# Reordering the mixers of a two-block network: linear attention among the gates' products, neighbourhood attention among Fourier mixing, gates by tanh, and dilated attention by pairs of units

## The chip, the cores and the metric

The kernel runs on one core of one Trainium2 chip. The metric is the device time of one execution in microseconds. Three runs of the kernel before took 4348.62 to 4350.44 us, median 4348.97 us.

## The reference, cut to what matters

Two blocks follow each other on a sequence of 2048 tokens of width 1024, all in float32. The first block is run twice (two layers, each with its own weights, on the 2048 latent tokens and 256 context tokens); the second block is run once.

```python
# first block, one layer
h   = rmsnorm(x, norm_w) * (1 + scale) + shift               # 2048 latent + 256 context tokens
f, fg, nq, nk, nv, ng, gq, gk, gv, gg, zf, zb = split(h @ w_in)
na   = neighbourhood_attention(nq, nk, nv, ctx_k, ctx_v, rpb) # 6 heads, 8x16 window + 256 context keys
gla  = gla_out_norm(gla_scan(forward) + gla_scan(backward))   # 4 heads, chunks of 64, gate logsigmoid/16
four = real(fft2(f, over positions and channels)) @ w_four
x    = x + gate * (concat(four * silu(fg), na * silu(ng), gla * silu(gg)) @ w_out)
# second block
q, k, v, gate_b, u, v_a, gate_a = split(rmsnorm(x) @ w_in_2)
o = dilated_attention(rope(norm(q)), rope(norm(k)), v)        # 8 heads, 3 dilations 1, 4, 16, merged by log-sum-exp
x = x + concat(o * silu(gate_b), gmlp(u, v_a) * silu(gate_a)) @ w_out_2
x = x + sigmoid(rmsnorm(x) @ w_ple_gate + b) * (p @ w_ple_proj)
```

## The kernel before

Every product is done in float32 as three fp32r products of high and low halves (`MM3`). The program is a sequence of Python generators. Each `yield` is a step, and a caller interleaves the steps of two or three generators; the framework's scheduler then fixes one instruction order per engine, and each engine takes its instructions in that order. Tiles come from pools with a fixed number of buffers; the attention scores, transposes and outputs live in PSUM banks.

A layer of the first block runs in stages. `b1_inproj` does the input projection. `mixers` (line 1318) then starts `Gates.steps` (line 558), a generator of 54 steps in layer 1 and 48 in layer 2, each one 24 products of 128x256 (`gps`, line 578) followed by a Silu on ScalarE (line 580). In this kernel two gate steps are taken after each step of `fourier` (22 steps in layer 1, 19 in layer 2; its products are named `fps`). Then the linear attention `Gla.steps` runs, 114 steps: three steps make one loop for one direction and one tile of 128 tokens (`gc` cumulative gates, `gT` transposes, `ga` masked scores, `gu` state updates, `go` outputs, `gpt` the transposes of a finished tile). The remaining gate steps go among the first 15 of these. After them the gates' memory is released and the neighbourhood attention `na` starts, one of its steps beside each further step of linear attention. Three `na` steps make one unit (128 queries of a pair of heads: `sc` and `sl` scores, `pc` and `pl` transposes, `po` values). The `na` steps left over run beside `ple_proj` (`plt`, `plo`) and the loads of `w_out`, and `OutProj` follows.

In `b2_attn`, the second block's attention, a unit is 128 queries of a head pair; there are 38 units for each of 4 head pairs, 16 with dilation 1, 14 with dilation 4 and 8 with dilation 16. `scores` (line 1783) makes two products that fill the array (line 1796) and two half-height ones (line 1799) per unit or part of a unit; VectorE adds the mask and takes the extremum, ScalarE takes exp; `turned` transposes (`apt`), `values` multiplies by V (`apo`). `step` (line 1939) lets transposes trail scores by two units and values trail by two more. `gather` sends the statistics of two dilations through DRAM on SyncE's queue, and `combine` merges the three dilations, for three of the four head pairs on GpSimd.

Of the kernel before, what the change touches and what calls it, by code (L numbers as in the profile page):

```python
# [10 lines left out]
F32 = mybir.dt.float32  # L11
# [522 lines left out]
class Gates:  # L534
# [24 lines left out]
    def steps(s):  # L559
# [9 lines left out]
        for i, c in enumerate(s.order):  # L569
            h = H.pop(i)  # L570
            for b in range(3):
                st = ip.ev.tile([128, 512], F32, name="ev", tag="ev")
                for j in range(2):
                    ps = s.pp.tile([128, 256], F32, name="gps", tag="gps", bufs=s.nps)
                    n = 0
                    for k in range(8):
                        for x, y in MM3:
                            nc.tensor.matmul(ps.rearrange("p (t n) -> p t n", t=2), W[b][k][y][:, 128 * j:128 * j + 128], h[x][:, :, k], start=n == 0, stop=n == 23)  # L578
                            n += 1
                    nc.scalar.activation(out=st[:, 256 * j:256 * j + 256], in_=ps, func=AF.Silu)  # L580
# [242 lines left out]
class Gla:  # L823
# [6 lines left out]
    def __init__(g, K, A, l, S, p, pp, nps, need):  # L830
# [8 lines left out]
        g.nw = p.tile([128, 96], F32, name="nw")  # L839
        nc.sync.dma_start(g.nw, dap(A["gla_norm_w"], 96 * l, [[0, 128], [1, 96]]))  # L840
        g.oacc = p.tile([128, 16 if not g.full else 18, 384], F32, name="oacc")
        g.L, g.VS, g.qd, g.kd = {}, {}, {}, {}
# [259 lines left out]
def na(K, A, l, S, B, p, pp, nps):  # L1102
# [99 lines left out]
    def turned(pr, g, j, st, es):  # L1202
# [6 lines left out]
        tcx = p.tile([128, 4, 128], F32, name="tcx", tag="tE", bufs=4)  # L1209
        nc.scalar.activation(out=tcx, in_=pc, func=AF.Copy)  # L1210
        tl = []
# [37 lines left out]
    def finish(pr, g, st):  # L1249
# [9 lines left out]
        ds = p.tile([8, 128], F32, name="ds", tag="ds", bufs=2)  # L1259
        if local:  # L1260
            nc.vector.tensor_copy(ds, dap_sb(pd, 127, [[-1, 128]]))
        else:
            nc.vector.tensor_copy(ds[:2 * n], pd[:2 * n])
        w = 128 * n
# [53 lines left out]
def mixers(K, A, l, S, B, ple, keep, proj):  # L1318

    tc = K.tc  # L1320

# [7 lines left out]
    with ExitStack() as es:  # L1329
# [7 lines left out]

        with ExitStack() as e1:
            for _ in fourier(K, A, l, S, pool(e1, "fo"), pool(e1, "fops", space=PSUM), 4):
                for _ in range(2):  # L1340
                    next(gates)
        w = proj.weights()
        with ExitStack() as e1:
# [3 lines left out]
            left = 3 * ((54 if l == 0 else 48) + 2)  # L1347
            for i, _ in enumerate(gla):
                if units is not None:
                    left -= 1  # L1350
                    next(units, None)
                elif i % 3 == 2 and [x for x in range(2) if next(gates, 1)]:
                    e2.close()
                    keep.close()
                    units = na(K, A, l, S, B, pool(es, "na", side="right"), pp, (2, 3))
                    next(units)
                    pp.tile = pool(es, "naps", space=PSUM, side="right").tile
        next(w)
        with ExitStack() as e1:
# [380 lines left out]
def b2_attn(K, A, S, p, pa, pq, pp):  # L1740
# [41 lines left out]

    def scores(pr, br, u, X):
        full = u[0][1] > 0
        st = X["st"]
        ps = pp.tile([128, 2, 512], F32, name="aps", tag="aps", bufs=2)
        ec = pa.tile([128, 2, 256], F32, name="ae", tag="ae", bufs=4)

        parts = [(u[0], u[0][1] - 1, slice(0, 256))] if full else [(x, 0, slice(128 * c, 128 * c + 128)) for c, x in enumerate(u)]

        early = (pr, br) == (0, 0) and u[0][1] < 4
        k0, q0, kl, k1, q1 = (K.first[:, i] for i in range(5)) if early else X["O"]
        for (r, b), b0, cs in parts:
            ks, qs = cols(br, r, b0, cs.stop - cs.start), cols(br, r, b, 128)
# [5 lines left out]
        for hh in range(2):  # L1800
            for (r, b), b0, cs in parts:

                col = (b, 4 * b + r, r)[br]
                m, d = (st[:, br, x, hh, col:col + 1] for x in range(2))
                nc.vector.tensor_tensor_reduce(out=ec[:, hh, cs], in0=ps[:, hh, cs], in1=band[:, cs if full else slice(128, 256)], scale=1.0, scalar=BIG,  # L1805
                                               op0=ALU.add, op1=ALU.min, accum_out=m)
                nc.scalar.activation(out=ec[:, hh, cs], in_=ec[:, hh, cs], func=AF.Exp, scale=-1.0, bias=m, accum_out=d)  # L1807
        return ec

    turn = [0]  # L1810

    def turned(pr, br, u, X, ec):
# [5 lines left out]
        et = pa.tile([128, 2, 2, 128], F32, name="aet", tag="aet", bufs=4)  # L1818
        turn[0] += 1
        if True:  # L1820
            nc.vector.tensor_copy(et[:, :, :n], pt[:, :, :n])
        else:
            nc.scalar.activation(out=et[:, :, :n], in_=pt[:, :, :n], func=AF.Copy)
        return et
# [22 lines left out]
    def gather(pr, X):  # L1847


        st = X["st"]  # L1850
        pst = pp.tile([64, 128], F32, name="pst", tag="apo", bufs=2)
# [3 lines left out]
        nc.vector.tensor_copy(sts, pst)  # L1855
        nc.sync.dma_start(sd[pr, 0].rearrange("s h (t n) -> (s h t) n", n=128), sts)
        for s_ in range(2):
            for hh in range(2):
                nc.sync.dma_start(dap(sd, ((pr * 2 + 1) * 4 + s_ * 2 + hh) * T, [[4, 128], [512, 4], [1, 4]]),
                                  st[:, 1, s_, hh].rearrange("p (b r) -> p b r", r=4))  # L1860
# [77 lines left out]

    def step(last=False):
        if len(B_) > 1 or last and B_:  # L1940
            last_, x = B_.pop(0)
            values(*x)
            if last_ and x[0] < 3:
                late.append(combine(x[0], x[3]))
        if len(A_) > 2 or last and A_:
            last_, x = A_.pop(0)
            B_.append((last_, x[:4] + (turned(*x),)))

    for i, (pr, br, n, u) in enumerate(units):
        X = Xs[pr]  # L1950
# [11 lines left out]
        if ahead and n % 2 == 0:  # L1962
            next(ahead, 1)
        A_.append((br == 2 and n == 7, (pr, br, u, X, scores(pr, br, u, X))))
        step()
# [6 lines left out]
    n = 0  # L1972
    while A_ or B_:
        step(True)
        if n < 3:
            next(last)
            n += 1
        yield
    yield True
# [409 lines left out]
```

## Time and profile before

| | us |
|---|---|
| median of 3 runs | 4348.97 |
| profiled execution, its own time | 4356.57 |
| its span, first to last instruction | 4354.8 |
| TensorE busy in the span | 4114.8 |
| VectorE busy | 1755.5 |
| ScalarE busy | 1649.8 |
| GpSimd busy | 1485.4 |

The mean granted TensorE clock is 0.956 of full speed. Busy time of TensorE is modelled, so a busy engine is not an engine at its peak. The profiled execution is 7.6 us above the median of the runs. In the rows below, PE is TensorE's products, PEld its weight loads, DVE VectorE, ACT ScalarE, POOL GpSimd, and times are counted from the start of the span.

### The profile page before, as it was taken

What the parts mean: (1) busy time and instruction counts of PE and PEld (TensorE: products, weight loads), DVE (VectorE), ACT (ScalarE), POOL (GpSimd) and SP (SyncE); (2) the same over time, 40 slices, a digit from 0 to 9 for tenths busy, and PEclk for the clock granted to TensorE, in tenths of its full rate; (3) what the DMA queues carried; (4) which work ended last, traced back from release to release, by engine and by line L of the source; (5) the groups of instructions that cost most, each with busy time, mean ns of one, the idle gap of its engine ahead of it and who ended that gap; (6) DMA issues with size and microseconds to landing.
All of it is one profiled execution on the core that took longest, in us unless ns stands there. A gap on an engine that the chain in (4) does not pass through costs nothing. (4 is left out here: it accounts for less than half of the span.)

```text
span 4354.8 us, 79569 instructions
## 1 busy us (share of the span) xinstructions
PE 4114.8 (94%) x29633; PEld 3510.3 (81%) x29633; DVE 1755.5 (40%) x4996; ACT 1649.8 (38%) x4121; POOL 1485.4 (34%) x1925
## 2 busy tenths in 40 slices
PE   7999999898899999999988989999999989998998
PEld 6988789676677799888967767889998867776887
DVE  5331123477532443112357744544620036665222
ACT  5141233574551333323355554251222125663121
POOL 4234333224222323232311422445723330643433
PEclk8999999898999999999989989999999988988999
DMA  6435444766766444434477674542321266745231
GB/s 206 138 112 150 145 162 152 190 166 182 201 188 209 140 142 126 123 120 158 150 201 178 165 203 153 170 126 76 107 89 50 87 194 141 174 107 162 84 92 63
DMA packets 551196, 629.94 MB, mean 145 GB/s; under 512 B 130792, under 2 KB 430124, under 8 KB 547354
## 3 DMA queue, kind: packets, MB, share of 16 engines
q1 hardware_dynamic: 500474, 477.71, 39.4%
q0 software_dynamic: 38784, 129.08, 9.0%
q10 hardware_dynamic: 11552, 18.08, 1.2%
q8 instruction: 235, 3.85, 0.4%
q14 instruction: 151, 1.24, 0.1%
HBM read 424.26 MB, written 200.41 MB: 143 GB/s over the span
## 5 line engine op out<-in xcount | busy, mean ns | idle before, releaser
L301 PE MATMUL mm<-whi,hTh 128*128 128x304 f32 (+2 forms) x1424 | 420.2, 299 | 1.6 <-ACT hTh L221 1.5
L301 PE MATMUL mm<-wlo,hTh 128*128 128x304 f32 (+2 forms) x1424 | 417.6, 297 | 0.0
L301 PE MATMUL mm<-whi,hTl 128*128 128x304 f32 (+2 forms) x1424 | 380.5, 296 | 0.0
L254 POOL TENSOR_TENSOR wlo<-wraw,whi 128x128 fp32r<-128x128 f32 (+3 forms) x384 | 223.7, 610 | 402.7 <-ACT whi L253 369.6
L301 PE MATMUL mm<-whi,h2h 128*128 128x256 f32 x1024 | 292.3, 289 | 1.5 <-ACT h2h L221 1.5
L301 PE MATMUL mm<-wlo,h2h 128*128 128x256 f32 x1024 | 284.2, 282 | 0.0
L301 PEld LDWEIGHTS mm<-whi,hTh 128*128 128x128 f32 x1424 | 268.9, 189 | 3.2 <-ACT hTh L221 2.3
L301 PE MATMUL mm<-whi,h2l 128*128 128x256 f32 x1024 | 271.1, 282 | 0.0
L301 PEld LDWEIGHTS mm<-wlo,hTh 128*128 128x128 f32 x1424 | 268.7, 189 | 0.0
L301 PEld LDWEIGHTS mm<-whi,hTl 128*128 128x128 f32 x1424 | 256.4, 189 | 1.1 <-issue 1.1
L578 PE MATMUL gps<-gh,whi 128*128 128x256 f32 x816 | 233.4, 286 | 8.5 <-ACT gh L155 8.5
L578 PE MATMUL gps<-gh,wlo 128*128 128x256 f32 x816 | 232.0, 284 | 0.0
L578 PE MATMUL gps<-gl,whi 128*128 128x256 f32 x816 | 231.5, 284 | 0.0
L304 PE MATMUL mm<-hTh,whi 128*128 128x512 f32 x600 | 227.9, 381 | 0.0
L304 PE MATMUL mm<-hTh,wlo 128*128 128x512 f32 x600 | 227.0, 378 | 0.0
L304 PE MATMUL mm<-hTl,whi 128*128 128x512 f32 x600 | 226.4, 377 | 0.0
L1430 PE MATMUL ops<-owh,omh 128*128 128x512 f32 x544 | 215.3, 396 | 4.2 <-ACT omh L155 4.2
L1430 PE MATMUL ops<-owh,om 128*128 128x512 f32 x544 | 213.0, 392 | 2.0 <-POOL om L156 2.0
L1430 PE MATMUL ops<-owl,omh 128*128 128x512 f32 x544 | 212.9, 391 | 0.0
L253 ACT ACTIVATE whi<-wraw 128x128 fp32r<-128x128 f32 (+3 forms) x416 | 127.3, 357 | 208.4 <-DMA wraw<-in_w_in 187.3
L1807 ACT ACTIVATE ae<-ae,ast 128x256 f32<-128x256 f32 (+1 forms) x384 | 171.1, 448 | 69.2 <-DVE ast L1805 69.2
L301 PEld LDWEIGHTS mm<-wlo,h2h 128*128 128x128 f32 x1024 | 195.7, 191 | 0.0
(483 smaller groups left out, 10893.4 us busy)
## 6 DMA issues: line engine op xcount, KB each, us to landing
qkv<-gl SPq DMA_DIRECT2D x72, 384.0 KB
adaw<-in_w_ada SPq DMA_DIRECT2D x48, 512.0 KB
Q<-ql SPq DMA_DIRECT2D x88, 256.0 KB
hl<-evk SPq DMA_DIRECT2D x68, 256.0 KB
gl<-hl SPq DMA_DIRECT2D x17, 1024.0 KB
om<-mixTl SPq DMA_DIRECT2D x34, 512.0 KB
gTl<-ev POOLq DMA_DIRECT2D x67, 256.0 KB, 3.1
wraw<-in_w_in SPq DMA_DIRECT2D x32, 512.0 KB
```

Of the source, the lines that this page charges most:

```text
L253: nc.scalar.activation(out=hi[:, :C], in_=raw[:, k], func=AF.Copy)
L254: (eng or nc.gpsimd).tensor_tensor(out=lo[:, :C], in0=raw[:, k], in1=f(hi[:, :C]), op=ALU.subtract)
L301: nc.tensor.matmul(ps[:, :C], s.hT[x][:, k, 128 * g:128 * g + 128], w[k][y][:, :C], start=st, stop=sp)
L304: nc.tensor.matmul(ps[:C, :tn], w[k][y][:, :C], s.hT[x][:, k, t0:t0 + tn], start=st, stop=sp)
L578: nc.tensor.matmul(ps.rearrange("p (t n) -> p t n", t=2), W[b][k][y][:, 128 * j:128 * j + 128], h[x][:, :, k], start=n == 0, stop=n == 23)
L1430: nc.tensor.matmul(ps, m[x][:, k], W[k][y][:, 512 * n:512 * n + 512], start=k == j == 0, stop=k == 7 and j == 2)
L1807: nc.scalar.activation(out=ec[:, hh, cs], in_=ec[:, hh, cs], func=AF.Exp, scale=-1.0, bias=m, accum_out=d)
```

## The change

Five things change. `Gates.steps` computes tanh(x/2) on ScalarE and then (tanh + 1) x on VectorE, which is twice the Silu; the factor one half is put into the linear attention's norm weight and into the neighbourhood attention's reciprocal denominators. In `mixers` the linear attention comes first with five gate steps for nine of its own, and the neighbourhood attention, begun when the gates are done, runs its steps beside the end of the linear attention, then beside Fourier mixing (4 steps per Fourier step in layer 1, 3 in layer 2), then beside `ple_proj`. While it is without linear attention (`K.alone`), one of its three evictions per unit goes to VectorE. In `b2_attn` two units share each pair of score tiles, all array-filling products stand before all half-height ones, and transposes and values follow by couples. The loads and stores of `gather` move from SyncE's queue to GpSimd's.

```diff
@@ Gates.steps
-                    nc.scalar.activation(out=st[:, 256 * j:256 * j + 256], in_=ps, func=AF.Silu)
+                    th = ip.ev.tile([128, 256], F32, name="gth", tag="ev")
+                    nc.scalar.activation(out=th, in_=ps, func=AF.Tanh, scale=0.5)
+                    nc.vector.scalar_tensor_tensor(out=st[:, 256 * j:256 * j + 256], in0=th, scalar=1.0, in1=ps, op0=ALU.add, op1=ALU.mult)
@@ Gla.__init__
+        nc.gpsimd.tensor_scalar(out=g.nw, in0=g.nw, scalar1=0.5, scalar2=None, op0=ALU.mult)
@@ na, turned
-        nc.scalar.activation(out=tcx, in_=pc, func=AF.Copy)
+        if K.alone:
+            nc.vector.tensor_copy(tcx, pc)
+        else:
+            nc.scalar.activation(out=tcx, in_=pc, func=AF.Copy)
@@ mixers
-        with ExitStack() as e1:
-            for _ in fourier(K, A, l, S, pool(e1, "fo"), pool(e1, "fops", space=PSUM), 4):
-                for _ in range(2):
-                    next(gates)
-        w = proj.weights()
+        K.alone = False
...
-                elif i % 3 == 2 and [x for x in range(2) if next(gates, 1)]:
+                elif i % 9 in (0, 2, 3, 5, 6) and next(gates, 1):
...
+        K.alone = True
+        w = proj.weights()
+        span = 4 if l == 0 else 3
+        with ExitStack() as e1:
+            for _ in fourier(K, A, l, S, pool(e1, "fo"), pool(e1, "fops", space=PSUM), 3):
+                for _ in range(span):
+                    left -= 1
+                    next(units, None)
@@ b2_attn, scores
-    def scores(pr, br, u, X):
+    def scores(pr, br, us, X):
-        ps = pp.tile([128, 2, 512], F32, name="aps", tag="aps", bufs=2)
+        ps = [pp.tile([128, 2, 256], F32, name="aps", tag="aps", bufs=4) for _ in range(2)]
...
+        for n, (i, _, (k0, q0, kl, k1, q1), r, b, cs, ks, qs) in enumerate(todo):
             for hh, (k, q) in enumerate(((k0, q0), (k1, q1))):
-                nc.tensor.matmul(ps[:, hh, cs], q[:, qs], k[:, ks], start=True, stop=False, skip_group_check=True)
+                nc.tensor.matmul(ps[hh][:, i, cs], q[:, qs], k[:, ks], start=n == 0, stop=False, skip_group_check=True)
+        for i, _, (k0, q0, kl, k1, q1), r, b, cs, ks, qs in todo:
             for hh, q in enumerate((q0, q1)):
                 h = slice(64 * hh, 64 * hh + 64)
-                nc.tensor.matmul(ps[:, hh, cs], q[h, qs], kl[h, ks], start=False, stop=True, skip_group_check=True)
+                nc.tensor.matmul(ps[hh][:, i, cs], q[h, qs], kl[h, ks], start=False, stop=True, skip_group_check=True)
@@ b2_attn, gather
-        nc.sync.dma_start(x, sd[pr].rearrange("b s h (i c) -> i (b s h) c", c=16))
+        nc.gpsimd.dma_start(x, sd[pr].rearrange("b s h (i c) -> i (b s h) c", c=16))
@@ b2_attn, step and its loop
-        if len(B_) > 1 or last and B_:
+        if B_:
...
-        if len(A_) > 2 or last and A_:
+        if len(A_) > 1 or done:
...
+        couple.append(u)
+        if n % 2:
+            A_.append((br == 2 and n == 7, [(pr, br, u, X, e) for u, e in zip(couple, scores(pr, br, couple, X))]))
+            couple = []
+            step()
-        if late and i % 2:
+        if late and n % 2 and (br or n > 5):
```

On ScalarE, in layer 1 where gate steps and linear attention run together, the kernel before has these rows (`ev<-gps` is the gate's Silu, `e<-gc` the linear attention's exp, `gT` its transposes):

```order
L580 ACT_TABLE_LOAD
L580 ACTIVATE ev<-gps 128x256
L934 ACT_TABLE_LOAD
L934 ACTIVATE e_8345<-gc 128x192
L935 ACTIVATE e_8346<-gc 128x192
L936 ACTIVATE e_8347<-gc 128x192
L941 ACTIVATE dec<-gc 48x2x2 x2
L1010 ACTIVATE oacc<-go 128x384
```

At such a place the changed kernel has these (`gth<-gps` is the gate's tanh):

```order
L965 ACTIVATE kT<-gT 128x256
L582 ACTIVATE gth<-gps 128x256
L155 ACTIVATE gh<-gl 128x1024 x2
L938 ACTIVATE e_6615<-gc 128x192
L939 ACTIVATE e_6616<-gc 128x192
L940 ACTIVATE e_6617<-gc 128x192
L945 ACTIVATE dec<-gc 48x2x2 x2
L582 ACTIVATE gth<-gps 128x256
```

The two table loads per gate step are gone from this place; the gate's tanh now stands between the exps of one loop and the copies of another.

On TensorE, in layer 1, the neighbourhood attention stands among the linear attention before:

```order
L1208 MATMUL pc<-ident,el 128x128 x4
L1217 MATMUL pl<-ident,el 80x128 x8
L1175 MATMUL sc<-Ks,Q 128x256
L1176 MATMUL sc<-Ks,Q 128x256
L1182 MATMUL sl<-Ks,Q 128x320
L1183 MATMUL sl<-Ks,Q 128x320
L1175 MATMUL sc<-Ks,Q 128x256
L1176 MATMUL sc<-Ks,Q 128x256
L975 MATMUL ga<-L_7910,kT 64x64 x8
L991 MATMUL gu<-qkv,ke 48x96 x8
L1235 MATMUL po<-tcx,vc 64x128 x2
L928 MATMUL gc<-la,tri 64x192 x4
```

In the changed kernel it stands among Fourier products (`fps`):

```order
L1186 MATMUL sl<-Ks,Q 128x440
L1212 MATMUL pc<-ident,el 128x128 x2
L1180 MATMUL sc<-Ks,Q 128x256
L1187 MATMUL sl<-Ks,Q 128x440
L1212 MATMUL pc<-ident,el 128x128 x2
L1242 MATMUL po<-tcx,vc 64x128 x4
L1265 MATMUL pd<-ident,dx 4x128
L750 MATMUL fps<-twh,ush 128x128 x2
L750 MATMUL fps<-twl,ush 128x128
L750 MATMUL fps<-twh,usl 128x128
```

The instructions of a unit are the same; what stands between them, and so what TensorE does while ScalarE and VectorE work on the unit, is other work.

On TensorE in the second block's attention the kernel before has these rows for the last unit of dilation 4 and the start of dilation 16 (`aps` scores, `apo` values, `apt` transposes); every unit of dilations 1 and 4 stands so:

```order
L1796 MATMUL aps<-kq 128x256 x2
L1799 MATMUL aps<-kq 128x256 x2
L1837 MATMUL apo<-aet,aV 64x128 x4
L1817 MATMUL apt<-ident,ae 128x128 x4
L1796 MATMUL aps<-kq 128x128 x2
```

The changed kernel has this for a couple of units of dilation 1:

```order
L1811 MATMUL aps<-kq 128x256 x4
L1815 MATMUL aps<-kq 128x256 x4
L1848 MATMUL apo<-aet,aV 64x128 x4
L1832 MATMUL apt<-ident,ae 128x128
L1848 MATMUL apo<-aet,aV 64x128 x4
L1832 MATMUL apt<-ident,ae 128x128 x7
```

The same products stand in groups twice as long, so there are half as many changes from one kind of product to the next.

## Rows read from the trace of the kernel before

**Rows 1.** Stage windows: length, then busy (count) of engines, clock, DMA share, GB/s.

```profile
core 0: us, PE busy (x) PEld busy (x) DVE busy (x) ACT busy (x) POOL busy (x), PEclk, DMA share, GB/s
578.00:747.00 169.00, 161.32 (x1258) 157.69 (x1258) 51.67 (x85) 65.00 (x139) 51.09 (x38) 0.96 0.52 168
800.50:822.00 21.50, 8.82 (x152) 6.61 (x152) 9.94 (x35) 7.96 (x22) 14.34 (x21) 0.88 0.90 204
822.00:1128.00 306.00, 278.79 (x3402) 224.09 (x3404) 213.01 (x792) 174.29 (x495) 100.18 (x136) 0.92 0.69 175
1128.00:1277.00 149.00, 130.00 (x1012) 101.61 (x1009) 61.54 (x198) 94.40 (x209) 17.86 (x24) 0.94 0.71 194
2202.60:2222.00 19.40, 13.08 (x185) 9.74 (x186) 11.55 (x36) 7.54 (x25) 8.83 (x15) 0.76 0.96 237
2222.00:2528.00 306.00, 273.61 (x3355) 221.79 (x3355) 204.48 (x767) 171.09 (x482) 94.41 (x128) 0.91 0.67 174
2528.00:2671.00 143.00, 121.83 (x902) 95.40 (x902) 56.80 (x178) 85.86 (x182) 14.86 (x19) 0.91 0.68 189
3555.00:3945.00 390.00, 378.38 (x2589) 286.74 (x2588) 240.72 (x952) 235.35 (x936) 136.00 (x157) 0.85 0.61 144
```

**Rows 2.** Windows, gate products (gps) on TensorE alone: busy (count), clock, DMA, GB/s.

```profile
747.00:763.00 16.00, 15.72 (x132) 1.00 0.77 254
784.90:799.20 14.30, 7.72 (x49) 1.00 0.72 210
```

**Rows 3.** Windows of the Fourier stages, Fourier products (fps) on TensorE alone.

```profile
578.00:747.00 169.00, 40.40 (x236) 0.96 0.52 168
2010.00:2156.00 146.00, 33.56 (x200) 0.98 0.54 173
```

**Rows 4.** Window 1177 to 1262: na transposes (pc), then ple products (plo), on TensorE.

```profile
1177.00:1262.00 85.00, 9.93 (x57) 1.00 0.71 191
...
1177.00:1262.00 85.00, 15.86 (x54) 1.00 0.71 191
```

**Rows 5.** The same window, all engines, columns as in rows 1.

```profile
1177.00:1262.00 85.00, 82.30 (x688) 65.82 (x687) 41.30 (x134) 62.94 (x137) 8.52 (x11) 1.00 0.71 191
```

**Rows 6.** Timeline, TensorE, a na unit's pieces: start, length, instruction [idle before].

```profile
2607.44 0.47 PE L1182 MATMUL sl<-Ks,Q 128*128 128x440 f32 x1
2607.75 0.37 PE L1183 MATMUL sl<-Ks,Q 128*128 128x440 f32 x1
2607.95 0.28 PE L1175 MATMUL sc<-Ks,Q 128*128 128x256 f32 x1
2608.07 0.28 PE L1176 MATMUL sc<-Ks,Q 128*128 128x256 f32 x1
2608.38 0.43 PE L1242 MATMUL po<-tl,vl 110*64 110x128 f32 x2
...
2609.82 1.09 PE L1242 MATMUL po<-tl,vl 110*64 110x128 f32 x14
2610.84 0.66 PE L1208 MATMUL pc<-ident,el 128*128 128x128 f32 x4
2611.33 1.04 PE L1217 MATMUL pl<-ident,el 128*110 128x128 f32 x8
2612.12 0.48 PE L1518 MATMUL plo<-plwh,plxsh 128*128 128x512 f32 x1
```

**Rows 7.** Groups by line, ScalarE: count, busy us, mean ns, idle before.

```profile
L1210 ACT ACTIVATE tcx<-pc 128x512 f32<-128x512 f32 x102 | 60.0, 588 | 34.0 <-PE pc L1208 33.9
L580 ACT ACT_TABLE_LOAD x8 | 10.3, 1283 | 0.1
L934 ACT ACT_TABLE_LOAD x7 | 9.0, 1283 | 2.6 <-PE gc L931 2.5
L936 ACT ACT_TABLE_LOAD x3 | 3.8, 1283 | 0.1
```

**Rows 8.** Timeline, TensorE, one unit of dilation 4 in the second block.

```profile
3793.62 0.66 PE L1817 MATMUL apt<-ident,ae 128*128 128x128 f32 x4
3794.03 0.81 PE L1796 MATMUL aps<-kq 128*128 128x256 f32 x2
3794.78 0.60 PE L1799 MATMUL aps<-kq 64*128 64x256 f32 x2
3795.30 0.66 PE L1837 MATMUL apo<-aet,aV 128*64 128x128 f32 x8
```

More of the change, by code (lines that the diff above doesn't have):

```diff
@@ L1259, in finish @@
         ds = p.tile([8, 128], F32, name="ds", tag="ds", bufs=2)
[L1260 to L1263, printed above, removed]
+        nc.vector.tensor_scalar(out=ds[:2 * n], in0=dap_sb(pd, 127, [[-1, 128]]) if local else pd[:2 * n], scalar1=0.5, scalar2=None, op0=ALU.mult)
         w = 128 * n
@@ L1781, in b2_attn @@
              [((r, 0), (r + 1, 0)) for r in range(0, 16, 2)]]
-    def scores(pr, br, u, X):
-        full = u[0][1] > 0
+    def scores(pr, br, us, X):
         st = X["st"]
-        ps = pp.tile([128, 2, 512], F32, name="aps", tag="aps", bufs=2)
[L1787 to L1794, printed above, removed]
+        ps = [pp.tile([128, 2, 256], F32, name="aps", tag="aps", bufs=4) for _ in range(2)]
+        ecs = [pa.tile([128, 2, 256], F32, name="ae", tag="ae", bufs=4) for _ in us]
+        todo = []
+        for i, u in enumerate(us):
+            full = u[0][1] > 0
+            parts = [(u[0], u[0][1] - 1, slice(0, 256))] if full else [(x, 0, slice(128 * c, 128 * c + 128)) for c, x in enumerate(u)]
+            early = (pr, br) == (0, 0) and u[0][1] < 4
+            O = [K.first[:, i] for i in range(5)] if early else X["O"]
+            todo += [(i, full, O, r, b, cs, cols(br, r, b0, cs.stop - cs.start), cols(br, r, b, 128)) for (r, b), b0, cs in parts]
+        for n, (i, _, (k0, q0, kl, k1, q1), r, b, cs, ks, qs) in enumerate(todo):
@@ L1800, in scores @@
-        for hh in range(2):
-            for (r, b), b0, cs in parts:
+                nc.tensor.matmul(ps[hh][:, i, cs], q[h, qs], kl[h, ks], start=False, stop=True, skip_group_check=True)
+        for i, full, _, r, b, cs, _, _ in todo:
+            for hh in range(2):
                 col = (b, 4 * b + r, r)[br]
                 m, d = (st[:, br, x, hh, col:col + 1] for x in range(2))
-                nc.vector.tensor_tensor_reduce(out=ec[:, hh, cs], in0=ps[:, hh, cs], in1=band[:, cs if full else slice(128, 256)], scale=1.0, scalar=BIG,
+                e = ecs[i][:, hh, cs]
+                nc.vector.tensor_tensor_reduce(out=e, in0=ps[hh][:, i, cs], in1=band[:, cs if full else slice(128, 256)], scale=1.0, scalar=BIG,
@@ L1806, in scores @@
                                                op0=ALU.add, op1=ALU.min, accum_out=m)
-                nc.scalar.activation(out=ec[:, hh, cs], in_=ec[:, hh, cs], func=AF.Exp, scale=-1.0, bias=m, accum_out=d)
-        return ec
-    turn = [0]
+                nc.scalar.activation(out=e, in_=e, func=AF.Exp, scale=-1.0, bias=m, accum_out=d)
+        return ecs
     def turned(pr, br, u, X, ec):
@@ L1818, in turned @@
         et = pa.tile([128, 2, 2, 128], F32, name="aet", tag="aet", bufs=4)
[L1819 to L1823, printed above, removed]
+        nc.vector.tensor_copy(et[:, :, :n], pt[:, :, :n])
         return et
@@ L1855, in gather @@
         nc.vector.tensor_copy(sts, pst)
-        nc.sync.dma_start(sd[pr, 0].rearrange("s h (t n) -> (s h t) n", n=128), sts)
+        nc.gpsimd.dma_start(sd[pr, 0].rearrange("s h (t n) -> (s h t) n", n=128), sts)
         for s_ in range(2):
             for hh in range(2):
-                nc.sync.dma_start(dap(sd, ((pr * 2 + 1) * 4 + s_ * 2 + hh) * T, [[4, 128], [512, 4], [1, 4]]),
+                nc.gpsimd.dma_start(dap(sd, ((pr * 2 + 1) * 4 + s_ * 2 + hh) * T, [[4, 128], [512, 4], [1, 4]]),
                                   st[:, 1, s_, hh].rearrange("p (b r) -> p b r", r=4))
         x = X["x"] = p.tile([128, 8, 16], F32, name="ax", tag="ax", bufs=1)
-        nc.sync.dma_start(x, sd[pr].rearrange("b s h (i c) -> i (b s h) c", c=16))
+        nc.gpsimd.dma_start(x, sd[pr].rearrange("b s h (i c) -> i (b s h) c", c=16))
     def combine(pr, X):
@@ L1937, in b2_attn, with step @@
     A_, B_, late = [], [], []
-    def step(last=False):
-        if len(B_) > 1 or last and B_:
[L1941 to L1944, printed above, removed]
-        if len(A_) > 2 or last and A_:
-            last_, x = A_.pop(0)
-            B_.append((last_, x[:4] + (turned(*x),)))
+    def step():
+        if B_:
+            last_, xs = B_.pop(0)
+            for x in xs:
+                values(*x)
+            if last_ and xs[0][0] < 3:
+                late.append(combine(xs[0][0], xs[0][3]))
+        if len(A_) > 1 or done:
+            if A_:
+                last_, xs = A_.pop(0)
+                B_.append((last_, [x[:4] + (turned(*x),) for x in xs]))
+    done, couple = [], []
     for i, (pr, br, n, u) in enumerate(units):
@@ L1963, in b2_attn @@
             next(ahead, 1)
-        A_.append((br == 2 and n == 7, (pr, br, u, X, scores(pr, br, u, X))))
-        step()
-        if late and i % 2:
+        couple.append(u)
[4 more added lines that the diff above has]
+        if late and n % 2 and (br or n > 5):
             if next(late[0], 1):
@@ L1972, in b2_attn @@
     n = 0
+    done.append(1)
     while A_ or B_:
[L1974 to L1978, printed above, removed]
+        step()
+        for _ in range(2):
+            if n < 3:
+                next(last)
+                n += 1
+            yield
     yield True
```

## The prediction

> **What bounds the kernel now.** I read the windows by stage first, then single pieces of work in the timeline, then the groups of ScalarE. The reader is to see in the windows that TensorE is busy for 161.3 of 169 us while Fourier products run among gate products, for 278.8 of 306 and 273.6 of 306 us while linear attention runs beside neighbourhood attention, and for 130.0 of 149 and 121.8 of 143 us in the stage beside the ple products; no other engine is over 213 of 306 [rows 1]. So TensorE's own work sets the time nearly everywhere, and reordering can only win what is idle (27, 19, 32 and 21 us in those four stages) and what runs at the lower clock: a mean grant of 0.92 means that 0.16 of a 306 us stage, 49 us, ran at 1.2 instead of 2.4 GHz. The second block's attention is busy 378 of 390 us at a grant of 0.85 [rows 1].
>
> I cut the mixers of layer 1 at 578 to 1277 us (699 us) and those of layer 2 at 2010 to 2671 (661 us), and rebuild each from prices.
>
> **Prices.** A gate product costs 16.0/132 = 0.121 us [rows 2]; a gate step has 24 of them. From 784.9 to 799.2 two loops of linear attention and 49 gate products took 14.3 us with almost no wait, so a loop costs (14.3 - 49 x 0.121)/2 = 4.2 us beside gates [rows 2]. Beside neighbourhood attention a step of linear attention, with the step of na next to it, took 306/99 = 3.09 us (114 steps less the 15 with gates) [rows 1]. Fourier's products are 40.4 and 33.6 us [rows 3]. A na unit beside ple: 57 transposes pc, four per unit, are 14.25 units in 85 us; less the 15.9 us in which ple products were busy, (85 - 15.9)/14.25 = 4.85 us, or 5.1 if a fifth of that time overlaps other work (an estimate) [rows 4]. Its pieces on TensorE alone add up to this: pc 0.49, pl 0.79, the 24 parts of po at 1.02 per 14 make 1.75, and two heads of scores sl and sc at 0.31 + 0.20 + 0.12 + 0.31 = 0.94 each make 1.88, in all 4.9 us; with the shortest of the score times, 0.2 and 0.12, it is 4.3 [rows 6]. So a unit costs at most 5.1 and at least 4.3 us, wherever it stands.
>
> **The mixers, stage by stage.**
> 1. Linear attention among gates. 54 gate steps at five of nine need 97 steps, 32.3 loops: 32.3 x 4.2 = 136 us, and 54 x 24 x 0.121 = 157 us. The transposes of finished tiles, which the priced window hasn't, and the start add 14 us (an estimate: the first stage was idle for 7.7 us before [rows 1], and now three loops of linear attention stand ahead of the first gate product, each waiting on ScalarE and VectorE). Layer 1: 307 us. Layer 2, 48 gate steps in 86 steps: 28.7 x 4.2 + 139 + 14 = 273.
> 2. The start of na, when its first loads wait for the gates' memory: 21.5 and 19.4 us before with TensorE busy 8.8 and 13.1 [rows 1]. It comes in the same place behind the last gate, so I keep 22 and 20.
> 3. Linear attention beside na: of 17 and 28 steps the first three lie in that start; 14 x 3.09 = 43 and 25 x 3.09 = 77 us.
> 4. na among Fourier: 88 and 57 steps are 29.3 and 19 units. The trace does not show this pair. Bounds are 4.3 and 5.1 us for a unit, with Fourier's products on top; I take 4.8, near the pieces' sum, since one eviction of 588 ns per unit leaves ScalarE [rows 7], which was busy for 62.9 of 85 us [rows 5]. 29.3 x 4.8 + 40.4 = 181 and 19 x 4.8 + 33.6 = 125 us.
> 5. na beside ple: 63 steps instead of 69 in layer 1, 65 instead of 51 in layer 2, and 0.3 us less for each unit: 149 - 10 - 6 = 133 and 143 + 22 - 6 = 159 us.
>
> Layer 1: 307 + 22 + 43 + 181 + 133 = 686 against 699. Layer 2: 273 + 20 + 77 + 125 + 159 = 654 against 661. Together 20 us less. That is little because the work is kept: what linear attention wins beside dense products, no wait and the full clock, is partly spent again where na loses its cover of gates.
>
> **Tanh.** 18 table loads of 1283 ns [rows 7] become two: 16 x 1.28 = 20.5 us of ScalarE. They lie in the stretch with gates, where TensorE had gate products to run, so I give them nothing; without this edit five gate steps among nine steps would have put a load before and behind nearly every one. New are 102 VectorE operations of 128x256 out of PSUM. The nearest row is a ScalarE eviction of 588 ns for twice the columns; at 0.3 to 0.6 us each they are 30 to 60 us on an engine that linear attention leaves mostly idle. They hold back the gate's PSUM bank, of which there are four; should that cover go, each gate step would wait for one such operation, 0.4 us, 41 us in all.
>
> By the Trainium skill (ScalarE: Activation LUTs, What ACT_TABLE_LOAD costs) a change of set costs 2.66 us with the drain that goes with the load. By that the removal would be 16 x 2.66 = 43 us of ScalarE, against 20.5 by the row; both are beside TensorE's work, so neither enters the sum.
>
> **The second block's attention.** In dilation 4 a unit takes 2.27 us: two array-filling products 0.75, two half-height ones 0.52, values 0.59, transposes 0.41, with no idle time between [rows 8]. All pieces stay. What can shrink is the half-height pair when another such pair follows it instead of the values: from 0.52 to at best the 0.375 of one array-filling product, 0.15 us per couple. A couple of full units has one such place (56 couples), one whose units have two parts has three (20 couples): 116 places x 0.15 = 17 us at best, nothing at worst. I take 8. The larger prize is the clock (a grant of 0.85 is 117 us at half speed), but the same products with the same strides give no reason for another clock; I give it nothing.
>
> By the Trainium skill (TensorE: Matmul & The Clock Gate, Part 3, what overlaps and what doesn't) a weight load overlaps a running product only when their row groups differ; pairs of half height that alternate between the upper and lower rows would then load under each other, and the 17 us would be had. The trace has no two such pairs in a row.
>
> Moving gather's DMAs to GpSimd puts them behind combine's products for the head pair before; the last combine waits for them. GpSimd is busy for 136 of 390 us in this stage [rows 1], so I cost it at nothing; if its queue is full just then, the length of a few of its operations, up to 10 us, appears in front of the tail's last products (an estimate).
>
> **Sum.** 20 + 8 = 28 us off the profiled execution's 4356.6. The median of the runs is 7.6 us lower; the same difference off 4349.0 gives 4321, and I say 4320.
>
> **Rivals.**
> A. The waits go as well. Beside Fourier's wide products na and linear attention keep the full clock, and idle time in the four na stages, 100 us in all, halves; a third of the 148 us that those stages spent at half speed is regained at half its length (25 us); couples get their 17 us. 4349 - 50 - 25 - 17 = 4257. For it: linear attention beside gates ran at a grant of 1.00 [rows 2]. Against it: idle time at the starts of stages has its own causes, loads behind released memory, and these remain.
> B. Nothing is left: na costs the full 5.1 us per unit beside Fourier and ple (0.3 x 91 units = 27 us back). 4349. For it: ScalarE, 63 of 85 us busy, gets Fourier's splits in addition.
> C. Slower: Fourier's chain becomes the wait. Each Fourier step loads, splits on ScalarE and then VectorE, and multiplies; TensorE takes its instructions in order, so a Fourier product whose half is late stops na too. Before, 48 independent gate products (5.8 us) stood between; now it is 1.3 units whose own exps sit ahead of the splits on ScalarE. At 2 us for each of the 41 Fourier steps this is 82 us: 4349 - 28 + 82 = 4403; from 0.7 us per step it eats the gain. Against it: before, this stage shows 7.7 us idle in all [rows 1].
> D. That the edit of the eviction does not do what it says (the wait moves with it from ScalarE to VectorE) is inside B.
>
> **How the numbers follow.** Forecast 0.50, with its own range 4285 to 4342; A 0.25; B 0.12; C 0.13, whose time is spread from 4350 upward. Two in ten left out at the ends gives 4245 to 4356: 0.09 below, out of A, and 0.10 above, out of C. A measurement of this kernel tells about 0.2%, 9 us: faster 0.77 (forecast nearly whole, A, a little of B), same 0.11, slower 0.12.
>
> **What would show it.** In the profile after: first stage near 300 us at a grant near 1.00, TensorE busy over 95%; no table loads between gates and exps; na among Fourier near 180 and 125 us. The clock in the second block's attention stays near 0.85 and the stage near 382 us. If Fourier products show long idle time before them, released by ScalarE or VectorE, it is C; if the na stages show under 5 us idle, A. The forecast is wrong if the first stage takes over 330 us: then linear attention's price beside gates was read from too short a stretch.

## The result and the profile after

The changed kernel takes 4376.73 us (median of four runs, 4370.39 to 4384.33) against 4348.8: 1.0061 of the time before, interval 1.0048 to 1.0074, so 28 us slower where 28 us faster was forecast. Its profiled execution took 4370.39 us, 13.8 more than that of before; it is the fastest of its four runs, while that of before lies above all its timed ones.

The stage windows of the changed kernel, columns as in [rows 1]; first layer 1 (start, linear attention among gates, start of `na`, linear attention beside `na`, Fourier, ple), then the same six of layer 2, then the second block's attention:

```profile
578.50:607.00 28.50, 15.25 (x157) 10.91 (x156) 12.40 (x34) 10.45 (x29) 5.02 (x13) 0.59 0.65 187
607.00:890.60 283.60, 274.45 (x3271) 244.22 (x3273) 175.27 (x537) 110.72 (x335) 119.38 (x128) 0.99 0.49 152
890.60:907.70 17.10, 9.82 (x139) 7.32 (x140) 11.21 (x44) 4.66 (x17) 9.92 (x16) 0.71 0.80 189
907.70:973.00 65.30, 44.98 (x422) 34.75 (x423) 31.17 (x126) 21.94 (x55) 28.16 (x38) 0.76 0.83 183
973.00:1163.50 190.50, 176.12 (x1418) 146.14 (x1417) 112.31 (x332) 109.94 (x255) 18.66 (x25) 0.93 0.66 183
1163.50:1302.30 138.80, 121.00 (x960) 94.31 (x958) 73.46 (x214) 80.33 (x178) 15.21 (x20) 0.93 0.71 195
2040.00:2068.80 28.80, 7.61 (x82) 4.82 (x81) 11.07 (x29) 5.89 (x13) 4.81 (x13) 0.58 0.69 191
2068.80:2312.20 243.40, 237.28 (x2817) 211.76 (x2818) 141.46 (x424) 96.83 (x293) 89.31 (x92) 0.99 0.49 152
2312.20:2330.00 17.80, 9.50 (x163) 7.26 (x162) 13.51 (x54) 5.68 (x20) 11.14 (x17) 0.94 0.78 180
2330.00:2419.00 89.00, 70.17 (x803) 57.44 (x804) 57.94 (x226) 42.41 (x112) 44.05 (x60) 0.88 0.84 205
2419.00:2551.50 132.50, 126.47 (x972) 104.44 (x972) 81.52 (x228) 78.24 (x179) 12.33 (x15) 0.92 0.75 204
2551.50:2694.90 143.40, 135.25 (x1103) 105.54 (x1103) 79.08 (x233) 88.00 (x192) 12.87 (x16) 0.99 0.69 199
3583.80:3960.20 376.40, 326.40 (x2573) 269.21 (x2573) 224.38 (x943) 228.22 (x933) 151.16 (x178) 0.87 0.59 147
```

Layer 1's mixers grew from 699 to 724 us, layer 2's fell from 661 to 655, and the second block's attention, 386 us from its first to its last product before, takes 376. The last stage of before, cut the same way, reads:

```profile
3557.00:3943.50 386.50, 375.73 (x2572) 284.55 (x2572) 238.48 (x944) 232.57 (x932) 133.57 (x154) 0.85 0.61 144
```

So TensorE is busy 49 us less than before, but idle for 50 of 376 us. Its timeline shows where: three long waits, at the end of three of the four head pairs.

```profile
3670.19 1.12 PE L1848 MATMUL apo<-aet,aV 128*64 128x128 f32 x8 [7.36 <-ACT aoT L1854]
...
3764.88 1.34 PE L1848 MATMUL apo<-aet,aV 128*64 128x128 f32 x10 [15.12 <-ACT aoT L1854]
...
3860.26 1.12 PE L1848 MATMUL apo<-aet,aV 128*64 128x128 f32 x8 [18.48 <-ACT aoT L1854]
```

ScalarE's eviction `aoT` is not the cause: ScalarE stood behind exps that waited for VectorE. VectorE's timeline has the cause, `combine`'s first minimum, idle before it for `gather`'s load `ax`:

```profile
3666.22 0.19 DVE L1883 TENSOR_TENSOR amn<-ax 128x32 f32<-128x32 f32 x1 [9.92 <-DMA ax<-sd]
...
3760.88 0.19 DVE L1883 TENSOR_TENSOR amn<-ax 128x32 f32<-128x32 f32 x1 [19.00 <-DMA ax<-sd]
...
3856.26 0.19 DVE L1883 TENSOR_TENSOR amn<-ax 128x32 f32<-128x32 f32 x1 [21.02 <-DMA ax<-sd]
```

Two things met. The load was issued late: for the second and third head pair its stores stand on GpSimd's queue behind `combine`'s products for the pair before, and for the first, when GpSimd was free, it stood idle for 6.18 us, which the profile's list of waiters puts down to `gather`'s own store. GpSimd's rows for the first and the second pair:

```profile
3659.54 0.94 POOL L1874 DMA_DIRECT2D ax<-sd  x1 [6.18 <-issue]
...
3746.66 1.28 POOL L1936 TENSOR_TENSOR aoT<-aoT 128x512 f32<-128x512 f32 x1
3747.88 0.80 POOL L1871 DMA_DIRECT2D sd<-ast  x1
```

And for these three pairs the scheduler put the minimum ahead of the masks of three of dilation 16's four couples, so that everything behind it on VectorE waited with it. For the second and third pair that place is not new: in the kernel before, all minima but the first stand ahead of six of dilation 16's eight units, and the second waited 1.55 us there:

```profile
3737.50 1.29 DVE L1871 TENSOR_TENSOR amn<-ax 128x32 f32<-128x32 f32 x1 [1.55 <-DMA ax<-sd]
```

Over the tile `ax`, who waited for it (us, times), in the changed kernel:

```profile
  DVE amn L1883: 53.7, 4
```

and in the kernel before:

```profile
  DVE amn L1871: 9.4, 3
```

The couples themselves gave far more than forecast. The same part of the timeline as [rows 8], one couple of dilation 4 (two units):

```profile
3642.32 1.29 PE L1811 MATMUL aps<-kq 128*128 128x256 f32 x4
3643.54 0.84 PE L1815 MATMUL aps<-kq 64*128 64x256 f32 x4
3644.31 1.09 PE L1848 MATMUL apo<-aet,aV 128*64 128x128 f32 x16
3645.34 1.09 PE L1832 MATMUL apt<-ident,ae 128*128 128x128 f32 x8
3646.18 1.29 PE L1811 MATMUL aps<-kq 128*128 128x256 f32 x4
```

From one couple's start to the next is 3.86 us, against 2 x 2.27 = 4.54 [rows 8]. Start to start, four array-filling products take 1.22 us (two took 0.75) and four half-height ones 0.77 (two took 0.52).

### The profile page after: what moved, and what is told of

The parts are those of the page before. It is cut to its first block, busy times and chain, and to the rows that moved or that the text cites. A ratio compares the mean times of both kernels' runs of the same rounds, so it can differ in the third digit from the quotient of the medians.

```text
span 4368.6 us, 79668 instructions
## 1 busy us (share of the span) xinstructions
PE 4079.7 (93%) x29633; PEld 3489.4 (80%) x29633; DVE 1841.1 (42%) x5188; ACT 1586.7 (36%) x4015; POOL 1501.6 (34%) x1951
## 5 line engine op out<-in xcount | busy, mean ns | idle before, releaser
L578 PE MATMUL gps<-gh,whi 128*128 128x256 f32 x816 | 242.3, 297 | 5.1 <-ACT gh L155 4.4
L1202 ACT ACTIVATE el<-el,st 128x696 f32<-128x696 f32 (+2 forms) x204 | 168.3, 826 | 109.1 <-DVE st L1199 107.0
```

Of the source, the lines that this page charges most:

```text
L1202: nc.scalar.activation(out=e[:, :n], in_=e[:, :n], func=AF.Exp, scale=-1.0, bias=m[:, hh, mi:mi + 1], accum_out=den[:, hh, dj:dj + 1])
```

## The experiments

All ratios are to the kernel before. "Layer 1" below is the length of layer 1's mixers in the run's profile, from the last input product to the first output product; before it was 699 us.

**Which edit costs: gather, attention, mixers, tanh.**

```diff
@@ e1_gather_sp: the changed kernel with
-        nc.gpsimd.dma_start(x, sd[pr].rearrange("b s h (i c) -> i (b s h) c", c=16))
+        nc.sync.dma_start(x, sd[pr].rearrange("b s h (i c) -> i (b s h) c", c=16))
...
@@ e2_b2_alone_sp: the kernel before with b2_attn of e1_gather_sp
@@ e3_mixers_alone: the changed kernel with b2_attn of before
@@ e4_tanh_alone: the kernel before with the diffs of Gates.steps, Gla.__init__ and na's ds
```

> The changed kernel with gather's loads and stores on SyncE's queue again, nothing else undone. Theory Q: in the changed kernel VectorE reached combine's first operation (amn<-ax) early and stood there 9.9, 19.0 and 21.0 us for gather's load behind GpSimd's queue, and TensorE lost 7.4, 15.1 and 18.5 us = 41 us to it. On SyncE those waits fall to the 1.6 to 6.3 us of the kernel before: 4377 - 41 + 2 = about 4338 us, second block's attention about 337 us. Rival P: the waits belong to the couples (two units' masks and exps stand ahead of each value product, whatever the queue): they remain, about 4377 us.

Measured 1.0006 (0.999 to 1.0022): 24 us less than the changed kernel. Theory Q holds in kind, not in size: VectorE waited 22.6 us for `ax` instead of 53.7, and the stage took 355.5 us, not 337. Of the four minima only the first now stood three couples later on VectorE, and the last two couples earlier; the second and third stood where they had, and waited 6.2 and 5.3 us for an earlier load instead of 19.0 and 21.0.

> The kernel before with the change of the second block's attention alone (couples, step, later combine), gather on SyncE's queue. Theory Q: the stage was 386 us before and 376 with 41 us of stalls after, so 335 us without them: 4349 - 51 = about 4298 us. Rival P: the stalls are the couples' own and stay, 4349 - 10 = 4339 us. Rival K (clock): the stage's half-speed time, 113 us before and 61 after, was shortened only because stalls broke the dense stretch up; without stalls it comes back, at half its length 26 us: about 4324 us.

Measured 0.9941 (0.9922 to 0.9961), 26 us faster; the stage took 357 us. That is nearest to K's number, but mostly not by K's mechanism: of the 22 us above theory Q's 335, 16 are idle time (25 us where Q left 50 - 41 = 9), and TensorE's busy time is only 5 us longer.

> The changed kernel with the second block's attention of the kernel before; so tanh and the new order of the mixers alone. Theory M: the order costs what the two profiles show between the start and that attention, 26 us, and all of it is the order's: 4349 + 26 = about 4375 us. Rival N: the profile of the kernel before was 7.6 us over its median and a good part of the shift is spread of single runs; the order costs under 10 us: 4349 to 4359 us.

Measured 1.0086 (1.0066 to 1.0106), 37 us slower; layer 1 took 734 us. Theory M, and more than the changed kernel's own profile showed: the same order took 734 to 736 us in three further profiles (gather on SyncE, the late minimum and the half-height products behind), so the 724 of the changed kernel's profiled execution is its low end.

> The kernel before with the gates' tanh and its halves alone; orders as before. Theory Z: the table loads lay beside gate products, so nothing changes: 4349, within 6 us. Rival L: the 18 loads of 1.28 us, less the two that stay, were in the path: 4349 - 20 = 4329 us. Rival V: each gate step now waits for the VectorE operation that follows, 0.4 us for 102 of them: 4349 + 41 = 4390 us.

Measured 1.0008 (0.9993 to 1.0022): nothing, as forecast.

**Where the mixers lose.**

```diff
@@ e5_silu: e1_gather_sp with Silu and whole factors
+                    nc.scalar.activation(out=st[:, 256 * j:256 * j + 256], in_=ps, func=AF.Silu)
@@ e6_tcx_act: e1_gather_sp with
-        K.alone = True
+        K.alone = False
@@ e7_layer2_only: e1_gather_sp with mixers of before where l == 0
@@ e8_gates_ahead: e1_gather_sp with, ahead of the loop over gla
+            for _ in range(6):
+                next(gates)
@@ e12_start_only: e1_gather_sp with, for l == 0, those six and
-                elif i % 9 in (0, 2, 3, 5, 6) and next(gates, 1):
+                elif i % 2 == 0 and next(gates, 1):
```

> The changed kernel with gather on SyncE (1.0006 of the kernel before in its own run) and with the gates' Silu and their whole factors instead of tanh; the order of the mixers is the changed one. Theory T: a gate step among linear attention's steps puts a table load of 1.28 us before and behind it on ScalarE, 2 x 102 at most, about 150 loads where exps and gates alternate; they hold the exps and transposes' copies that TensorE waits for, so at least a quarter, 50 us, shows: ratio 1.012 or more. Rival: TensorE has gate products to run meanwhile and nothing shows: 1.0006, within 0.002.

Measured 1.004 (1.0025 to 1.0056), 15 us over the same kernel with tanh. The profile has 114 of the loads at the two alternating lines:

```profile
L934 ACT ACT_TABLE_LOAD x57 | 73.1, 1283 | 3.9 <-PE gc L931 2.9
L580 ACT ACT_TABLE_LOAD x57 | 73.1, 1283 | 3.2 <-issue 2.4
```

146 us of ScalarE showed as about 15 in the time: between the two theories, a tenth and not a quarter.

> The changed kernel with gather on SyncE and the eviction tcx on ScalarE everywhere. Theory T: beside Fourier mixing and ple ScalarE was busy 110 of 190.5 and 72 of 116 us with that eviction on VectorE; 48 and 40 units there get 0.59 us more of it, and at the 0.3 us a unit of the prediction the four stages lose 0.3 x 91 = 27 us: ratio 1.007. Rival: the unit's wait only moves between the two engines: 1.0006, within 0.002.

Measured 1.0011 (0.9997 to 1.0026): the rival. Moving that eviction to VectorE is worth nothing that can be told.

> The changed kernel with gather on SyncE, and layer 1's mixers in the order of before (tanh kept). Theory L: the loss is layer 1's alone, where the mixers went from 699 to 724 us (734 in the two experiments on the order and on gather), while layer 2's went from 661 to 655: 25 to 35 us back, ratio 0.993 to 0.995. Rival S: both layers lose alike and the difference between the profiles is spread: half the 37 us of the mixers alone, ratio 0.996 to 0.998.

Measured 0.992 (0.9902 to 0.9938): theory L. Layer 1 took 697 us and layer 2 656. The loss is layer 1's alone.

> The changed kernel with gather on SyncE, and six gate steps taken before linear attention's first step, so that the three loops that stood uncovered at the start of each layer's mixers run among gate products; the rest of the order follows from that. Theory U: the starts, 28.5 and 28.8 us with TensorE busy 15.3 and 7.6 at a clock of 0.59 and 0.58, shrink by their idle time and their half speed, about 12 + 7 and 20 + 4 us, less one late loop's wait in each: 30 to 40 us, ratio 0.992 to 0.994. Rival W: the waits are for loads that come when they come, and the gates that cover them are missing at the end, where na starts earlier among more steps of linear attention: at best 10 us, ratio 0.998 to 1.001.

Measured 0.9968 (0.9957 to 0.9979), 17 us faster than without; layer 1 fell to 701 us, but layer 2 went from 653 to 658. Theory U's saving came in layer 1 alone, where the six steps do two things: they cover the start, and they leave ten more steps of linear attention for `na`. The next run parts them.

> The changed kernel with gather on SyncE (1.0006), and in layer 1 six gate steps ahead of linear attention's first step and the other 48 spread at one for two, so that nearly as many steps of linear attention as before stand among gates (96 of 97) and only the start is covered. Theory U: the uncovered start is the loss: layer 1's mixers fall from 734 to about 717 us, ratio 0.997. Rival W: what six gate steps ahead won (0.9968, layer 1 at 701 us) came from the ten steps of linear attention that moved beside neighbourhood attention, where they cost nothing: layer 1 stays at 725 to 735, ratio 0.999 to 1.001.

Measured 0.997 (0.9956 to 0.9985); layer 1 at 720 us, 15 less: theory U. By the profiles, the other 19 us that `e8_gates_ahead` won in layer 1 go with the ten moved steps. Its two windows of layer 1, up to the last gate and from the start of `na` on:

```profile
579.10:863.40 284.30, 267.18 (x3192) 238.34 (x3193) 166.98 (x494) 113.81 (x337) 109.16 (x120) 0.98 0.52 158
...
881.40:1279.90 398.50, 349.23 (x3009) 281.42 (x3009) 231.74 (x733) 219.84 (x516) 77.15 (x102) 0.94 0.73 195
```

and those of `e12_start_only`:

```profile
579.60:885.00 305.40, 283.96 (x3421) 251.85 (x3421) 183.26 (x569) 119.94 (x360) 121.07 (x139) 0.97 0.53 158
...
901.70:1299.20 397.50, 347.48 (x2796) 280.09 (x2796) 219.09 (x671) 212.17 (x488) 62.12 (x84) 0.89 0.71 187
```

With 213 more products of linear attention beside `na`, that part took 398.5 instead of 397.5 us, at a grant of 0.94 instead of 0.89; the part with gates was 21 us shorter for them. In this pair of profiles the ten steps are nearly free beside `na` and paid in full beside gates. The times do not confirm it: the ratios of the two runs, 0.9968 and 0.997, agree within their intervals, and with layer 2 some 5 us longer in `e8_gates_ahead` they leave about 6 us for the ten steps (an estimate), not 19. Layer 2's profiles say the opposite (`e13_start_layer2`, below).

**What stalls and what wins in the second block's attention.**

```diff
@@ e10_minima_late: the changed kernel with
-        nc.vector.tensor_tensor(out=m2, in0=x[:, 0, 0], in1=x[:, 1, 0], op=ALU.min)
-        nc.vector.tensor_tensor(out=m2, in0=m2, in1=st[:, 0, 0], op=ALU.min)
+        nc.vector.tensor_tensor(out=m2, in0=x[:, 0, 0], in1=st[:, 0, 0], op=ALU.min)
+        nc.vector.tensor_tensor(out=m2, in0=m2, in1=x[:, 1, 0], op=ALU.min)
@@ e11_half_behind: e1_gather_sp, the half-height pair inside the first loop of scores
-        for i, _, (k0, q0, kl, k1, q1), r, b, cs, ks, qs in todo:
             for hh, q in enumerate((q0, q1)):
```

> The changed kernel, gather still on GpSimd's queue, with combine's first minimum taken between dilation 16's statistics and gather's first load, so that VectorE meets it three couples of dilation 16 later. Theory V: GpSimd's queue alone does no harm, the harm was that VectorE came to the wait with masks behind it; of 41 us of waits at least 30 go, less what the half-speed clock takes back: 20 us or more, ratio 1.0015 or less. Rival Q: the queue itself makes combine late and TensorE waits for it at another place: 1.006.

Measured 0.9981 (0.9967 to 0.9995), 35 us less than the changed kernel, with `gather` still on GpSimd. Theory V: the stage took 347 us.

> The changed kernel with gather on SyncE (1.0006) and the half-height products of each part put behind its own array-filling ones again; couples of transposes and values stay. Theory G: what the couples won, 47 us of TensorE's time in the stage, is a price of each change between kinds of products; a couple of dilation 4 has 6 changes instead of 4 (8 before), one of dilation 16 has 10 instead of 4; half of the gain or more, 23 to 38 us, goes: ratio 1.006 to 1.009. Rival H: only pairs of half-height products under each other won, at most the 17 us of the prediction: ratio 1.002 to 1.0045. Rival F: the gain came from fewer waits and another clock: 1.0006.

Measured 1.0119 (1.0104 to 1.0134): 49 us over the same kernel with the half-height products apart, beyond theory G. Its stage:

```profile
3595.00:3992.20 397.20, 392.83 (x2572) 300.60 (x2572) 224.16 (x943) 227.91 (x931) 131.66 (x149) 0.84 0.57 139
```

Its pairs of scores in dilation 4 cost what they cost before, 0.73 and 0.53 us from start to start (0.75 and 0.52 in [rows 8]):

```profile
3644.40 0.80 PE L1811 MATMUL aps<-kq 128*128 128x256 f32 x2
3645.13 0.60 PE L1814 MATMUL aps<-kq 64*128 64x256 f32 x2
3645.66 0.84 PE L1811 MATMUL aps<-kq 128*128 128x256 f32 x2
3646.43 0.60 PE L1814 MATMUL aps<-kq 64*128 64x256 f32 x2
3646.96 0.88 PE L1831 MATMUL apt<-ident,ae 128*128 128x128 f32 x6
```

So the whole gain is the grouping of scores by kind; couples of transposes and values give nothing without it. The stage was even 11 us longer than before, with TensorE busy for 17 us more; no run explains that.

**The best of both.** `e9_both` is `e7_layer2_only` with the late minimum; the two runs behind it settle what was open.

```diff
@@ e13_start_layer2: e9_both with e12_start_only's edit where l == 1
@@ e14_best_gather_pool: e9_both with gather on nc.gpsimd
```

> The kernel with layer 1 in the order of before, layer 2 in the changed order and gather on SyncE (0.992 in its own run), and combine's first minimum taken between dilation 16's statistics and gather's first load instead of between gather's two: VectorE then cannot meet it before dilation 16's masks are done. Theory V: with gather on SyncE VectorE still stood 5.2, 6.2, 5.3 and 5.9 us for that load and TensorE about 17 us for VectorE; they go: 0.988. Rival: the transposes and values stand still for other reasons there, or the half-speed clock takes the place: 0.992.

Measured 0.9884 (0.9869 to 0.99), 50 us faster than the kernel before: theory V. Only the minimum differs from `e7_layer2_only`, whose stage took 353.6 us:

```profile
3562.70:3899.10 336.40, 322.89 (x2573) 266.16 (x2573) 223.73 (x943) 228.40 (x932) 132.31 (x149) 0.92 0.71 165
```

> The best kernel so far (layer 1 in the order of before, layer 2 in the changed one, gather on SyncE, the late minimum; 0.9884 in its own run) with layer 2's start covered as layer 1's was: six gate steps ahead of linear attention's first step, the other 42 at one for two (84 steps of linear attention among gates instead of 86). Theory U: the uncovered start costs layer 2 what it cost layer 1, 15 us: its mixers go from 656 to about 641 us, ratio 0.985. Rival E: the start costs layer 2 nothing, since what follows na's start was 5 us longer there for the six steps ahead while it was 33 us shorter in layer 1: 656 us, ratio 0.988.

Measured 0.9882 (0.9864 to 0.9899), layer 2 at 656 us: rival E. The part up to the last gate was 15 us shorter (255 against 270), and what follows 15 us longer (401 against 386). Why layer 2 gives it back and layer 1 doesn't, stays open. Its layer 2 up to the last gate, and from there on:

```profile
2002.60:2257.30 254.70, 237.88 (x2842) 212.16 (x2843) 143.60 (x439) 100.46 (x298) 88.45 (x100) 0.98 0.54 162
2257.30:2658.20 400.90, 354.85 (x3091) 282.60 (x3089) 232.82 (x754) 217.87 (x510) 85.32 (x113) 0.92 0.73 195
```

and that of `e8_gates_ahead`, which has the same six gate steps ahead in layer 2 and nine more steps of linear attention beside `na`:

```profile
2018.10:2258.20 240.10, 225.64 (x2636) 202.92 (x2637) 129.11 (x374) 95.12 (x277) 77.42 (x84) 0.98 0.53 158
2258.20:2676.30 418.10, 367.75 (x3298) 293.66 (x3297) 246.48 (x816) 223.20 (x534) 99.50 (x129) 0.91 0.74 195
```

The nine steps took 14.6 us off the part with gates and put 17.2 us on the part behind it: in layer 2 they were not free beside `na`.

> The best kernel so far (0.9884) with gather on GpSimd's queue, as in the changed kernel; so all of the change but the order of layer 1's mixers, plus the late minimum. Theory V: VectorE's place was the whole harm: 0.988 to 0.989. Rival Q: GpSimd's queue costs by itself what the attention stages of the two experiments with the late minimum differ by, 347 against 336 us: 0.991.

Measured 0.9886 (0.9869 to 0.9903): theory V. The attention stage took 343 us, 7 more than on SyncE, of which the time shows nothing.

## Why the prediction was wrong

**The mixers of layer 1: the failed step.** Forecast 307 + 22 + 43 + 181 + 133 = 686; the windows show 312 + 17 + 65 + 190.5 + 139 = 724. The price of linear attention beside gates held (312 against 307 us, 316 to 322 in four other profiles of this order), and the start of `na` took less than forecast. What failed first is step 3, 14 steps at a mean of 3.09 us. That mean was taken over 99 steps, and the first loops beside `na` cost more in both kernels. Linear attention's `gc` in two stretches before, the start of `na` and the even run behind it (16 products are one loop):

```profile
802.60:854.20 51.60, 6.02 (x64) 4.00 (x64) 4.46 (x20) 0.77 1.01 222
865.20:996.80 131.60, 19.14 (x258) 13.24 (x258) 17.83 (x80) 0.96 0.64 172
```

and the start of `na` after:

```profile
899.10:947.70 48.60, 3.08 (x34) 1.92 (x34) 2.23 (x10) 0.61 1.00 204
```

A loop took 12.9 us at the start and 8.2 in the even run; after, 24 us, at a grant of 0.61 and with the DMA engines at their full share. TensorE's longest waits there are for `na`'s first loads and for VectorE:

```profile
907.72 0.55 PE L1179 MATMUL sc<-Ks,Q 128*128 128x256 f32 x1 [4.28 <-DMA Q<-ql]
...
916.60 0.55 PE L1179 MATMUL sc<-Ks,Q 128*128 128x256 f32 x1 [5.27 <-DMA Ks<-kl]
...
942.72 0.56 PE L995 MATMUL gu<-qkv,ke 64*48 64x96 f32 x4 [7.47 <-DVE ggt L1041]
```

The cost of the first loops was averaged over 99 steps, and the mean was then applied to 14 steps that are mostly first loops. In step 4 a unit among Fourier products cost (190.5 - 40.4) / 29.3 = 5.1 us, the upper bound and not the 4.8 taken; the reason for 4.8, the eviction that leaves ScalarE, is worth nothing (`e6_tcx_act`). Step 5 missed by 6.

Behind these sums stands an idea that did not carry. The prediction called TensorE's work the limit and moved linear attention to where it found dense company, although the gates were dense already without it. The new order costs layer 1 some 35 us, and the order of before gives them back (`e7_layer2_only`). Of these, 15 are the uncovered start (28.5 us at a grant of 0.59, TensorE busy for 15): covering it won them (`e12_start_only`). For the other 20 the cause stays open. That `na`, which waits by itself, misses linear attention as company is argued from one pair of layer 1's profiles; the times and layer 2 speak against it.

**The mixers of layer 2** came out at 655 us against a forecast of 654, by errors that cancel: steps 3 and 4 were 12 and 7 too low, step 5 16 too high. Why the order helps here stays open.

**The second block's attention** fell by 10 us against a forecast of 8, and both halves of the forecast were wrong. The term for couples was mis-sized, 8 us (at best 17) against 49 us less busy TensorE in this profile and 44 to 55 in those with couples grouped by kind: I let only a half-height pair gain, while array-filling products gained as much. And `gather` on GpSimd was costed at nothing because GpSimd is busy for only a third of the stage; its cover is not that share but the distance, on VectorE, between the load's issue and the first operation that reads it. I looked for the wait at the end of the tail, where 10 us were allowed, and not inside the stage, where TensorE lost 41 us behind a VectorE operation of 0.19 us. The order of VectorE's instructions in the kernel before, had it been read for this place, shows the minimum ahead of the masks in three of four head pairs.

By the Trainium skill (TensorE: Matmul & The Clock Gate, Part 3) weight loads run under a product only where the row groups differ. That half-height products cost half as much as array-filling ones once the price of a group is taken off (0.125 against 0.235 us, last section) agrees with it; the gain itself is that price, which both kinds pay alike and the rule does not speak of.

**What held.** Tanh at nothing (`e4_tanh_alone`), the need for it in the new order (`e5_silu`), linear attention's first stage, and no rival C: in layer 1 TensorE was busy 176 of 190.5 us among Fourier products. The sum, 28 us of gain, failed by layer 1's 38 us, by some 10 more in other executions, and by an attention stage that kept 10 of a possible 50.

## What to carry to other kernels

When independent work is to be moved, price it for the place where it will stand, and count the first loops of a stage by themselves instead of averaging them into a step. Whether such work is free beside a stage that waits has to be measured there: here layer 1's profiles say yes and layer 2's say no. When a load moves to another queue, read the order of the engine that consumes it, down to the first reader and what stands behind that reader; a late load with an early reader stops an in-order engine whatever the queue's mean load. Here an earlier load won 24 us of the time and a later reader 35. And group products of one kind, array-filling or half-height: here that was the largest gain in the whole change.

## What the runs showed of the hardware

A change between the two kinds of score products has a price of its own. Array-filling products take 0.75 us for two and 1.22 for four, half-height ones 0.52 and 0.77. Taken as a price for the group and one for each product, that is 0.28 + 2 x 0.235 and 0.27 + 2 x 0.125 us. The same four and four products take 1.99 us in two groups and 2.56 in four (`e11_half_behind`), 0.28 us for each group more.

With `gather` on SyncE, one minimum of 128x32 took 6.45 us instead of 0.19. VectorE's row, and GpSimd's beside it, in `e1_gather_sp`:

```profile
3752.20 6.45 DVE L1883 TENSOR_TENSOR amn<-ax 128x32 f32<-128x32 f32 x1 [6.22 <-DMA ax<-sd]
```

```profile
3751.19 2.53 POOL L1934 TENSOR_TENSOR aoT<-aoT,awb 128x512 f32<-128x512 f32 x2
3753.68 1.26 POOL L156 TENSOR_TENSOR x<-x 128x512 fp32r<-128x512 f32 x1
...
3757.34 1.25 POOL L1936 TENSOR_TENSOR aoT<-aoT 128x512 f32<-128x512 f32 x1
3758.54 0.58 POOL L1920 DMA_DIRECT2D agt<-g  x1
```

It ended when GpSimd's run of six operations did; at the same place it took 6.80 us in `e2_b2_alone_sp` and 6.67 in `e7_layer2_only`. By the Trainium skill (SBUF — State Buffer, SBUF: two separate sides) a VectorE operation with two inputs in that memory and a GpSimd operation that reads it exclude each other for a whole instruction. The row agrees, and adds that VectorE did not get in between six GpSimd operations in a row.
